# Handing an up projection over to its down projection: last column pair one tile at a time, its square and blocks in halves, a product moved forward

## The chip, the cores and the metric

The kernel runs on one core of one Trainium2 chip. The metric is the device time of one execution in microseconds. Engines are named as the profile names them: PE multiplies matrices (PEld is its weight load, which overlaps it), DVE and ACT work element by element, POOL is the general-purpose engine, SP issues most of the DMAs. Results of PE land in PSUM, in eight banks of 128 x 512 floats; the kernel names them a (two), b (two), c (two), d and e.

## The reference

A decoder trunk of two layers on 512 tokens of width 1024: a gated short convolution, then an MLP; a shared key and value side; sparse attention, then an MLP; a last normalization. The change touches the MLP alone:

```python
def squared_relu_mlp(h, w1, w2):
    return jnp.square(jax.nn.relu(h @ w1)) @ w2
```

`w1` is 1024 x 4096, `w2` 4096 x 1024, all in float32.

## The kernel before

**Numbers in two halves.** Every float32 operand is split into a float16 high half and a float16 low half. A product of two operands is three matmuls: high by high, low by high, high by low. `ACT.activation(..., AF.Copy)` makes the high half and a DVE subtraction makes the low half, for weights (`whi`/`wlo`, `wh`) as for activations (`rh` high, `rl` low).

**Stages of an MLP.** Each MLP handles the 4096 hidden channels in two halves, and each half is an up projection (`mlp_up`) followed by a down projection (`mlp_down`). So in the whole kernel there are four handovers from an up projection to a down projection: two in layer 0, two in layer 1.

**Up projection.** `mlp_up` (line 1010) goes over eight column pairs `p`. A pair is two tiles of 128 hidden channels by 512 tokens, each accumulated in its own PSUM bank. Most pairs are computed by `pair` (line 773): for each of eight chunks of the contraction it issues three matmuls for the first tile and three for the second, so both tiles are complete only at the end, after 48 matmuls of 512 columns. Its weights come as two pieces, one for chunks 0 to 3 and one for chunks 4 to 7. (In the second half some pairs, never the last one, are made by `seven` with seven products of half-size blocks.)

**`squares(p)`** (line 1023) turns a pair into what the down projection needs. DVE scales each tile and clips it at zero (`ml_t`, two instructions of 512 columns). ACT squares both in one instruction of 1024 columns (`ml_z`, blocks 0 to 3 of 256 columns: the two tiles by the two halves of the tokens). `sums_of` (line 454) makes blocks 4 to 7, differences of the first four, in three DVE instructions. Then one ACT copy of blocks 1 to 7 (1792 columns) makes `rh[:, p]`, and one DVE subtraction of 1792 columns makes `rl[:, p]`.

**Down projection.** The seven products of a Strassen-like scheme stand for the eight block products of a 2 x 2 by 2 x 2 multiplication. `PRODUCTS` (line 321) gives for each of the products 0 to 6 its weight block and its activation block: product 0 reads activation block 1, product 1 reads block 3, product 4 reads block 4. `mlp_down` (line 1062) goes over four column pairs. `product(i, ps, cs)` (line 1068) issues, for each chunk `c` of `cs`, three matmuls of 256 columns into bank `ps`; chunk `c` reads `rh[:, c]` and `rl[:, c]`, and so chunk 7 needs `squares(7)`, the last pair of the up projection. When `give` is set the product frees its weight block, and it then calls `ahead()`, which converts further weight pieces as far as there is room: the converted blocks lie in a ring of seven, and the eighth needs the tile of the first.

For the first down pair (line 1095) three products, 0 into bank a, 4 into bank c and 1 into bank d, run over chunks 0 to 6 first. After that chunk 7 of product 0 is issued, ACT copies the result of product 0 into the bank of W_ (bank b), chunk 7 of product 4 and of product 1 follow, and then product 2 accumulates on top of the copy in bank b.

**What sets the order.** The instructions of a stage are not issued as they are written. `Plan` records them as tasks, each numbered as the program came to it, with an estimated cost (`cost`) and its dependencies. `issue` (line 185) then simulates the engines and lists the tasks: on each engine, of the tasks that are ready or will be within a short look-ahead (60 ns on PE, 150 on DVE and ACT), the one with the lowest number is next. An engine that finds nothing of a low number ready takes a later task, for instance a weight conversion for a stage that comes much later; such tasks are called fillers below. The order that comes out is fixed: on the chip each engine runs its list strictly in order and waits at semaphores. Layer 0's MLP is one plan, attention another, layer 1's MLP a third.

Of the kernel before, what the change touches and what calls it, by code (L numbers as in the profile page):

```python
# [12 lines left out]
AF = mybir.ActivationFunctionType  # L13
OP = mybir.AluOpType
# [267 lines left out]
def body(ctx, tc, x, rel_bias, norm_mix, norm_mlp, mlp_w1, mlp_w2, a_w_in, a_conv_w, a_w_out,  # L282
# [4 lines left out]
    PE, ACT, DVE, POOL, SPQ = (plan.engine(e) for e in ("PE", "ACT", "DVE", "POOL", "SP"))  # L287
# [143 lines left out]
    def kind(i):  # L431
        shape = pieces[i][1]
        return "seven" if shape is None else "down" if shape[0] == "down" else "dense"

    def room(ring, n, more=1):
        return all(ring[-k]["done"] for k in range(n - more + 1, n + 1) if k <= len(ring))
# [187 lines left out]
    def next_piece():  # L624

        i = pos["use"]
        pos["use"] += 1
        while i not in ready:
            for _ in convert_piece():
                pass  # L630
        return ready.pop(i)

    def ahead():
        while pos["cv"] < len(pieces) and pos["cv"] < pos["use"] + AHEAD2[kind(pos["cv"])]:
            k = kind(pos["cv"])
            if k != "dense" and not room(halves, HALVES[0], 2 if k == "seven" else 1):
                return
            yield from convert_piece()

    def drain(gen):  # L640
        for _ in gen:
            pass


    first = tc.tile_pool(name="first", bufs=1)
# [122 lines left out]
    def mm3(ps, w, xs, start, stop):  # L768
        PE.matmul(ps, w[0], xs[0], start=start, stop=False)
        PE.matmul(ps, w[0], xs[1], start=False, stop=False)  # L770
        PE.matmul(ps, w[1], xs[0], start=False, stop=stop)

    def pair(xs, ps, kn=8, mid={}):

        for c in range(kn):
            if c % 4 == 0:
                if c:
                    drain(ahead())
                w = next_piece()
            if c in mid:  # L780
                mid[c]()
            for m in range(2):
                mm3(ps[m], [u[:, c % 4, m * 128:(m + 1) * 128] for u in w], [u[:, c] for u in xs],
                    c == 0, c == kn - 1)
# [12 lines left out]
    xs = new_split(wk[0], "x0")  # L797
# [80 lines left out]
    for p in range(4):  # L878
        pc, pu, pb = [], [], []
        if p == 0:  # L880
# [38 lines left out]
            ws = [next_piece(), next_piece()]  # L919
# [21 lines left out]
        for part, dst in ((1, pc), (2, pu), (0, pb)):  # L941
# [12 lines left out]
            for c in SUM_AT.get((p, part), ()):  # L954
                z = wk[0].tile([128, 8, 256], F32, name="sv_z", bufs=1)
                with plan.behind(first_lo[0]):
                    block_sums(c, "mix0", z, [sums[:, hl, 4 * c:4 * c + 4] for hl in range(2)])
            for m in range(2):
                ch = 2 * p + m
                if dst is pc:  # L960
                    if m == 0:
                        tmps = []
                    t = ftile("cv_t", 2)
# [23 lines left out]
    xs = new_split(work, "xs")  # L987
    ss = SumSq()
# [18 lines left out]
    ROOT_AT, ROWS_AT = 7, 1  # L1007
    SUMS_AT = (3, 4, 5, 6)

    def mlp_up(xs, ss, rh, half, rb, gname, kept):  # L1010
        turn[0], layer = 1, int(gname[-1])
        first = half == 0
        if not first:
            sums = [u[:, 5:8].rearrange("p a b n -> p (a b) n")[:, 0:16] for u in rh]
            for hl in range(2):
                POOL.dma_start(sums[hl], kept[:, hl])

        def rows():
            nonlocal rb
            rb = row_tile(broadcast_rows(ss.r), RD * math.sqrt(SR) / (SW * SX))  # L1020
            squares(0)

        def squares(p):
            ph = held[p]
            t = wk[0].tile([128, 2, S], F32, name="ml_t", bufs=2)
            if len(ph) == 3:
                lo, hi = slice(0, 256), slice(256, 512)
                DVE.scalar_tensor_tensor(t[:, :, lo], ph[0], 0.0, rb[:, None, lo].to_broadcast([128, 2, 256]),
                                         op0=OP.max, op1=OP.mult)
                for m in range(2):  # L1030
                    DVE.scalar_tensor_tensor(t[:, m, hi], ph[1 + m], 0.0, rb[:, hi], op0=OP.max, op1=OP.mult)
            else:
                for m in range(2):
                    DVE.scalar_tensor_tensor(t[:, m], ph[m], 0.0, rb, op0=OP.max, op1=OP.mult)
            z = wk[0].tile([128, 8, 256], F32, name="ml_z", bufs=2)
            ACT.activation(z[:, 0:4].rearrange("p (m k) n -> p m (k n)", m=2), t, AF.Square)
            sums_of(z)
            ACT.activation(rh[0][:, p], z[:, 1:8], AF.Copy)
            DVE.tensor_tensor(rh[1][:, p], z[:, 1:8], rh[0][:, p], op=OP.subtract)

        held = {}
        for p in range(8):
            if not first and p in UP7[layer]:
                dlo = wk[0].tile([128, 2, 256], F32, name="dn_w", bufs=1)
                held[p] = seven(xs, sums, dlo)
                drain(ahead())
                squares(p)
                continue
            held[p] = [acc(), acc()]
            pair(xs, held[p], mid={ROOT_AT: ss.rstd} if first and p == 0 else {ROWS_AT: rows} if first and p == 1 else {})  # L1050
            drain(ahead())
            if p or not first:
                squares(p)
            if first and p in SUMS_AT:
                c = SUMS_AT.index(p)
                z = wk[0].tile([128, 8, 256], F32, name="ml_z", bufs=2)
                block_sums(c, gname, z, [u[:, 7, 0:4] for u in rh])
                for hl in range(2):
                    SPQ.dma_start(kept[:, hl, 4 * c:4 * c + 4], rh[hl][:, 7, 0:4])
        return rb  # L1060

    def mlp_down(rh, done, mid=None, last=None):

        sc = 1.0 / (SR * SW2)
        n1, n2 = slice(256, 512), slice(0, 256)
        blocks = {}

        def product(i, ps, cs=range(8), more=False, give=True):
            own = more and len(cs) == 8
            a, b = PRODUCTS[i]  # L1070
            if i not in blocks:
                blocks[i] = next_piece()
            wh, wl, u = blocks[i]
            for c in cs:
                xh, xl = (r[:, c, b - 1] for r in rh)
                for n, (w, x_) in enumerate(((wh, xh), (wl, xh), (wh, xl))):
                    PE.matmul(ps, w[:, c], x_, start=not more and c == 0 and n == 0, stop=c == 7 and n == 2,
                              skip_group_check=own)
            if give:
                u["done"] = True  # L1080
            drain(ahead())

        for p in range(4):
            blocks.clear()
            if last and p == 3:
                return last(blocks, product)
            X1, X2 = X[:, 2 * p + 1], X[:, 2 * p]
            both = X[:, 2 * p:2 * p + 2, n2]
            X_, W_, V_ = (bank(g + str(p % 2))[:, 0:256] for g in "abc")

            def stt(o, ps):
                DVE.scalar_tensor_tensor(o, ps, sc, o, op0=OP.mult, op1=OP.add)

            u = wk[0].tile([128, 2, 256], F32, name="dn_w", bufs=1)
            if p == 0:
                Y_ = bank("d")[:, 0:256]
                for i, ps in ((0, X_), (4, V_), (1, Y_)):
                    product(i, ps, range(7), give=False)
                product(0, X_, (7,), True)
                ACT.activation(W_, X_, AF.Copy)  # L1100
                product(4, V_, (7,), True)
                ACT.activation(u[:, 0], V_, AF.Copy, scale=sc)
                product(1, Y_, (7,), True)
                stt(X1[:, n1], X_)
                stt(X1[:, n1], Y_)
            else:
                product(0, X_)
                ACT.activation(W_, X_, AF.Copy)
                product(4, V_)
                ACT.activation(u[:, 0], V_, AF.Copy, scale=sc)  # L1110
            if mid and p:
                mid(p)
            product(2, W_, more=True)
            ACT.activation(u[:, 1], W_, AF.Copy, scale=sc)
            product(5, V_, more=True)
            stt(X1[:, n2], V_)
            DVE.tensor_tensor(both, both, u, op=OP.add)
            product(3, W_, more=True)
            stt(X2[:, n2], W_)
            if p:  # L1120
                product(1, X_, more=True)
                stt(X1[:, n1], X_)
            product(6, W_, more=True)
            stt(X2[:, n1], W_)
            if done:
                drain(done(p))
# [12 lines left out]
    with pool("hidden_a") as hp:  # L1139
        wk[0] = hp  # L1140
        rh = first_half(hp, xs, ss, "mlp0")
        xkv = new_split(work, "xs")
        ss = SumSq()
# [12 lines left out]
    with pool("attn") as ap_:  # L1156
# [295 lines left out]
        og, parts, keep = {}, {}, {}  # L1452
# [260 lines left out]
        for i in range(len(items) + 6):  # L1713
# [11 lines left out]
            while credit > 0.0:  # L1725
                u = next(bg, "end")
# [17 lines left out]
    xs = xm  # L1744
    ss = ss2


    with pool("hidden_b") as hp:
        wk[0] = hp
        rh = first_half(hp, xs, ss, "mlp1")  # L1750
# [163 lines left out]
```

## Time and profile before

| | us |
|---|---|
| median of 3 runs | 1091.97 |
| lowest and highest of them | 1091.97, 1092.24 |
| the profiled execution, its own time | 1091.95 |
| its span, first to last instruction | 1090.2 |
| PE busy in the span | 1073.5 |
| DVE busy | 930.7 |
| ACT busy | 639.0 |

The time of the profiled execution is 1.75 us longer than its span; the profile shows only what lies in the span. Rows of the timeline give the start, the length, the engine, the line, the operation, output<-inputs by tile name, the shape and how many instructions were merged into the row; in brackets stands the engine's idle time before it and what ended it. Every instruction has line 242, since the planner issues them all from there, so the rows are told apart by tile names. The four handovers lie at about 256, 411, 850 and 1004 us of the span. Of the names: `c<-xs,whi` is an up matmul into bank c, `a<-rh,wh` and `a<-rl,wh` are down matmuls with the high and the low half of the activations, `ml_t<-c,rb` is the scaling in `squares`, `ml_z<-ml_t` its Square, `ml_z<-ml_z` its sums, `rh<-ml_z` its copy, `rl<-ml_z,rh` its subtraction, `b<-a` the copy into W_'s bank, `wh<-wst` a weight conversion.

### The profile page before, as it was taken

The page shows a single profiled execution, that of the slowest core. Times are in us where ns is not written, and L with a number is a line of the kernel's source. Part 1 is how long each engine was busy: PE and PEld are TensorE (multiplying, and loading weights), DVE is VectorE, ACT ScalarE, POOL GpSimd, SP SyncE. Part 2 cuts the span into 40 slices and gives each one's busy share as a digit, 9 for nine tenths or more (in the row PEclk, how much of TensorE's full clock was granted, in tenths as well). Part 3 has the DMA queues.
Part 4 walks back from the last instruction along what each step waited for, and adds up shares of the span by engine and source line. Part 5 has one row for each costly group of instructions (what it writes and reads, how often), then busy time and mean ns, then how long its engine had stood idle before and what let it go on. Part 6 is the DMA issues. An engine that isn't in the chain of part 4 may idle for free.

```text
span 1090.2 us, 21151 instructions
## 1 busy us (share of the span) xinstructions
PE 1073.5 (98%) x8442; PEld 736.7 (68%) x8442; DVE 930.7 (85%) x1574; ACT 639.0 (59%) x1082; POOL 68.4 (6%) x93
## 2 busy tenths in 40 slices
PE   9999999999999999999999999999999999999997
PEld 4457844446885758886766696775444788775887
DVE  7999987899986898958886889997879996699883
ACT  6655555566543565546766687865656543554552
POOL 2000000000000000000002122210000000000121
PEclk9999999999999999999999999999999999999999
DMA  8535698345425414215633352002834453431312
GB/s 273 174 106 171 231 286 278 112 155 156 136 78 174 147 47 137 77 37 152 195 116 117 99 194 67 22 21 76 233 117 136 135 155 107 153 119 45 112 40 78
DMA packets 159236, 143.45 MB, mean 132 GB/s; under 512 B 7853, under 2 KB 147841, under 8 KB 158625
## 3 DMA queue, kind: packets, MB, share of 16 engines
q1 hardware_dynamic: 155712, 132.60, 39.6%
q10 hardware_dynamic: 2464, 4.70, 1.3%
q0 software_dynamic: 960, 4.80, 1.2%
q8 instruction: 66, 1.08, 0.4%
q14 instruction: 34, 0.27, 0.1%
HBM read 123.55 MB, written 15.51 MB: 128 GB/s over the span
## 4 chain that ended last, share of the span: by engine, by line
PE 78%; DVE 16%; issue 2%; ACT 2%; DMA 1%; SPq 0%; POOL 0%; POOLq 0%; DVEq 0%; ACTq 0%
PE b L242 28%; PE a L242 26%; PE c L242 20%; DVE ml_z L242 3%; DVE rl L242 3%; PE d L242 3%; DVE ml_t L242 3%; DVE wh L242 3%; DVE wlo L242 2%; PE e L242 1%; ACT rh L242 1%; DVE wst L242 1%; DMA wst<-a_w_in_dram 1%; ACT ml_z L242 0%; DVE at_s L242 0%
## 5 line engine op out<-in xcount | busy, mean ns | idle before, releaser
L242 PEld LDWEIGHTS <-wh 128*128 128x128 f16 x3648 | 356.3, 98 | 54.6 <-ACT wh L242 4.8
L242 PEld LDWEIGHTS <-whi 128*128 128x128 f16 x1664 | 159.9, 98 | 165.2 <-issue 1.8
L242 PE MATMUL b<-rh,wh 128*128 128x256 f16 x904 | 151.6, 273 | 0.5 <-ACT b L242 0.5
L242 ACT ACTIVATE whi<-wst 128x1024 f16<-128x1024 f32 (+5 forms) x122 | 103.1, 858 | 76.5 <-PE b L242 29.5
L242 PEld LDWEIGHTS <-wlo 128*128 128x128 f16 x832 | 81.4, 98 | 88.9 <-DVE wlo L242 0.6
L242 ACT ACTIVATE wh<-wst 128x1024 f16<-128x1024 f32 (+1 forms) x108 | 106.3, 1005 | 59.7 <-PE b L242 32.9
L242 DVE SCALAR_TENSOR_TENSOR wlo<-wst,whi 128x1024 f16<-128x1024 f32 (+5 forms) x122 | 118.1, 980 | 24.4 <-ACT whi L242 24.3
L242 DVE SCALAR_TENSOR_TENSOR wh<-wst,wh 128x1024 f16<-128x1024 f32 (+1 forms) x108 | 123.3, 1164 | 5.0 <-ACT wh L242 3.2
L242 PE MATMUL b<-rl,wh 128*128 128x256 f16 x452 | 123.2, 273 | 0.0
L242 PE MATMUL a<-xs,whi 128*128 128x512 f16 (+1 forms) x384 | 103.1, 355 | 0.1
L242 PE MATMUL b<-xs,whi 128*128 128x512 f16 x320 | 95.3, 379 | 0.0
L242 PE MATMUL c<-rh,wh 128*128 128x256 f16 x552 | 93.6, 273 | 0.0
L242 ACT ACTIVATE at_p<-at_s,at_m 128x128 f32<-128x128 f32 (+3 forms) x128 | 71.0, 556 | 29.0 <-DVE at_m L242 27.1
L242 ACT ACTIVATE rh<-ml_z 128x1792 f16<-128x1792 f32 (+1 forms) x40 | 62.7, 1567 | 42.2 <-DVE ml_z L242 42.2
L242 DVE TENSOR_TENSOR rl<-ml_z,rh 128x1792 f16<-128x1792 f32 (+1 forms) x40 | 74.4, 1861 | 15.1 <-ACT rh L242 15.0
L242 PE MATMUL c<-xs,whi 128*128 128x512 f16 x288 | 86.0, 379 | 0.0
L242 ACT ACTIVATE wh<-ml_t 128x1024 f16<-128x1024 f32 x48 | 50.6, 1054 | 48.7 <-DVE ml_t L242 45.5
L242 PE MATMUL a<-rh,wh 128*128 128x256 f16 x432 | 73.3, 273 | 3.7 <-ACT wh L242 3.7
L242 PE MATMUL c<-rl,wh 128*128 128x256 f16 x276 | 75.2, 273 | 0.0
L242 DVE CUSTOM_DVE_ANT_0 at_s<-b,T 128x128 f32<-128x128 f32 (+3 forms) x128 | 59.1, 485 | 15.1 <-PE b L242 14.4
L242 PE MATMUL a<-xs,wlo 128*128 128x512 f16 (+1 forms) x192 | 67.4, 355 | 0.0
L242 DVE TENSOR_TENSOR ml_z<-ml_z 128x256 f32<-128x256 f32 (+1 forms) x120 | 61.5, 512 | 5.1 <-ACT ml_z L242 2.2
(294 smaller groups left out, 2004.7 us busy)
## 6 DMA issues: line engine op xcount, KB each, us to landing
wst<-mlp_w_dram SPq DMA_DIRECT2D x32, 1024.0 KB, 5.4
wst<-mlp_w_dram SPq DMA_DIRECT2D x100, 256.0 KB, 3.8
early<-pre_hl SPq DMA_DIRECT2D x14, 512.0 KB, 3.6
wst<-mlp_w_dram SPq DMA_DIRECT2D x48, 128.0 KB, 2.7
wst<-a_w_in_dram SPq DMA_DIRECT2D x20, 256.0 KB, 4.0
wst<-w_kv_dram SPq DMA_DIRECT2D x10, 512.0 KB, 4.0
T<-ext_d ACTq DMA_DIRECT2D x4, 1056.0 KB, 6.1
wst<-a_w_in_dram SPq DMA_DIRECT2D x8, 512.0 KB, 5.0
```

The lines of the kernel that those rows point to most:

```text
L242: getattr(self.engines[t["e"]], t["op"])(*t["args"], **t["kw"])
```

## The change

Three edits, all at the handover. A new function `pair_in_turn` takes both weight pieces of the pair at its start and issues all 24 matmuls of the first tile and then all 24 of the second; further weight conversions are recorded after the fourth chunk of each. `mlp_up` uses it for `p == 7`.

For `p == 7` `squares` makes the Square in two instructions of 512 columns, one for each tile. The ACT copy is made in two parts: blocks 1 to 3 ahead of `sums_of`, blocks 4 to 7 after it. The DVE subtraction is split in the same way, and both of its parts are recorded after `sums_of`.

In `mlp_down`, for the first down pair, products 0 and 4 run over chunks 0 to 6, then chunk 7 of product 0, ACT's copy into W_, product 1 over all eight chunks, and only then chunk 7 of product 4.

```diff
+    def pair_in_turn(xs, ps):
+
+        ws = [next_piece(), next_piece()]
+        for m in range(2):
+            for c in range(8):
+                if c == 4:
+                    drain(ahead())
+                mm3(ps[m], [u[:, c % 4, m * 128:(m + 1) * 128] for u in ws[c // 4]], [u[:, c] for u in xs],
+                    c == 0, c == 7)
...
-            ACT.activation(z[:, 0:4].rearrange("p (m k) n -> p m (k n)", m=2), t, AF.Square)
+            for k in [slice(m, m + 1) for m in range(2)] if p == 7 else [slice(0, 2)]:
+                ACT.activation(z[:, 0:4].rearrange("p (m k) n -> p m (k n)", m=2)[:, k], t[:, k], AF.Square)
+            parts = (slice(1, 4), slice(4, 8)) if p == 7 else (slice(1, 8),)
+            if p == 7:
+                ACT.activation(rh[0][:, p, 0:3], z[:, 1:4], AF.Copy)
             sums_of(z)
-            ACT.activation(rh[0][:, p], z[:, 1:8], AF.Copy)
-            DVE.tensor_tensor(rh[1][:, p], z[:, 1:8], rh[0][:, p], op=OP.subtract)
+            for k in parts:
+                to = slice(k.start - 1, k.stop - 1)
+                if p < 7 or k.start == 4:
+                    ACT.activation(rh[0][:, p, to], z[:, k], AF.Copy)
+                DVE.tensor_tensor(rh[1][:, p, to], z[:, k], rh[0][:, p, to], op=OP.subtract)
...
-            pair(xs, held[p], mid={ROOT_AT: ss.rstd} if first and p == 0 else {ROWS_AT: rows} if first and p == 1 else {})
+            (pair_in_turn if p == 7 else pair)(xs, held[p], **{} if p == 7 else dict(mid={ROOT_AT: ss.rstd} if first and p == 0 else {ROWS_AT: rows} if first and p == 1 else {}))
...
-                for i, ps in ((0, X_), (4, V_), (1, Y_)):
+                for i, ps in ((0, X_), (4, V_)):
                     product(i, ps, range(7), give=False)
                 product(0, X_, (7,), True)
                 ACT.activation(W_, X_, AF.Copy)
+                product(1, Y_)
                 product(4, V_, (7,), True)
                 ACT.activation(u[:, 0], V_, AF.Copy, scale=sc)
-                product(1, Y_, (7,), True)
                 stt(X1[:, n1], X_)
                 stt(X1[:, n1], Y_)
```

## The prediction, made before the changed kernel was run

> **What bounds the kernel now.** The page comes first, for the engine that has no room; then the busy time by stretches, for the places where that engine does stand still; then the timeline of those places.
>
> ```profile
> span 1090.2 us, 21151 instructions
> PE 1073.5 (98%) x8442; PEld 736.7 (68%) x8442; DVE 930.7 (85%) x1574; ACT 639.0 (59%) x1082; POOL 68.4 (6%) x93
> ```
>
> ```profile
> 256.00:266.30 10.30, 8.72 (x76) 7.19 (x75) 10.23 (x13) 5.32 (x6) 0.00 (x0) 1.00 0.55 177
> 266.30:330.00 63.70, 63.70 (x584) 57.06 (x584) 58.59 (x75) 30.45 (x38) 0.00 (x0) 1.00 0.40 118
> 330.00:411.00 81.00, 81.00 (x509) 49.50 (x508) 68.41 (x87) 42.09 (x44) 1.15 (x2) 1.00 0.40 129
> 411.00:420.70 9.70, 8.69 (x76) 7.17 (x75) 8.34 (x12) 4.19 (x5) 0.00 (x0) 1.00 0.61 200
> ...
> 1004.00:1014.10 10.10, 9.00 (x78) 7.34 (x77) 7.08 (x10) 4.24 (x5) 0.00 (x0) 1.00 0.68 210
> ```
>
> The columns are the stretch, its length, then busy time and count of PE, PEld, DVE, ACT and POOL, then the granted clock, DMA share and GB/s. PE is the bound: in a down projection (266 to 330) and an up half (330 to 411) it is busy for every microsecond. The short stretches are the four handovers from an up projection to the first down pair; there PE loses time. A busy row counts a matmul's whole duration, which overlaps the next, so the loss is better read from starts:
>
> ```profile
> 263.53 0.38 PE L242 MATMUL d<-rh,wh 128*128 128x256 f16 x2
> 264.39 0.27 PE L242 MATMUL a<-rl,wh 128*128 128x256 f16 x1 [0.48 <-DVE rl L242]
> 264.50 0.27 PE L242 MATMUL c<-rl,wh 128*128 128x256 f16 x1
> 264.61 0.27 PE L242 MATMUL d<-rl,wh 128*128 128x256 f16 x1
> 265.81 0.28 PE L242 MATMUL a<-rh,wh 128*128 128x256 f16 x1 [0.93 <-ACT wh L242]
> 266.26 0.38 PE L242 MATMUL b<-rh,wh 128*128 128x256 f16 x2 [0.17 <-ACT b L242]
> ...
> 418.49 0.38 PE L242 MATMUL d<-rh,wh 128*128 128x256 f16 x2
> 418.96 0.27 PE L242 MATMUL a<-rl,wh 128*128 128x256 f16 x1
> ...
> 420.64 0.38 PE L242 MATMUL b<-rh,wh 128*128 128x256 f16 x2
> ...
> 857.60 0.38 PE L242 MATMUL d<-rh,wh 128*128 128x256 f16 x2
> 858.46 0.27 PE L242 MATMUL a<-rl,wh 128*128 128x256 f16 x1 [0.48 <-DVE rl L242]
> ...
> 860.33 0.38 PE L242 MATMUL b<-rh,wh 128*128 128x256 f16 x2 [0.17 <-ACT b L242]
> ...
> 1011.96 0.38 PE L242 MATMUL d<-rh,wh 128*128 128x256 f16 x2
> 1012.23 0.27 PE L242 MATMUL a<-rl,wh 128*128 128x256 f16 x1
> ...
> 1014.10 0.38 PE L242 MATMUL b<-rh,wh 128*128 128x256 f16 x2 [0.17 <-ACT b L242]
> ```
>
> ```profile
> 269.04 2.62 PE c L242 x24
> ...
> 194.22 10.36 PE a L242 x48
> ```
>
> 24 matmuls of 256 columns take 2.62 us, 0.109 each. Between the two quoted starts of a handover lie six of them, 0.66 us. So PE stands still for 2.73 - 0.66 = 2.07 us at the first handover, 2.15 - 0.66 = 1.49 at the second, 2.73 - 0.66 = 2.07 at the third, 2.14 - 0.66 = 1.48 at the fourth: **7.11 us in all**. It has two parts. The first wait, for the low halves `rl` of the last pair, is 264.39 - 263.75 = 0.64 at the first handover. The second (265.81 - 264.72 = 1.09, and 266.26 - 265.92 = 0.34) is for ACT, which first splits a weight block and only then copies X_ into W_'s bank. At the others the first wait is the distance from `d<-rh` to `a<-rl` less two matmuls, 0.47 - 0.22 = 0.25, 0.86 - 0.22 = 0.64 and 0.27 - 0.22 = 0.05. The second wait is the remainder: 1.43, 1.24, 1.43 and 1.43. Sums: 1.58 for the first wait, 5.53 for the second.
>
> **The change, part by part.** These are the two helpers at the first handover:
>
> ```profile
> 257.43 1.06 ACT L242 ACTIVATE ml_z<-ml_t 128x1024 f32<-128x1024 f32 x1 [3.01 <-DVE ml_t L242]
> ...
> 260.21 1.70 ACT L242 ACTIVATE rh<-ml_z 128x1792 f16<-128x1792 f32 x1 [0.59 <-DVE ml_z L242]
> 264.70 1.06 ACT L242 ACTIVATE wh<-wst 128x1024 f16<-128x1024 f32 x1 [2.79 <-PE a L242]
> ...
> 254.98 1.22 DVE L242 SCALAR_TENSOR_TENSOR wh<-ml_t,wh 128x1024 f16<-128x1024 f32 x1
> 256.12 1.28 DVE L242 SCALAR_TENSOR_TENSOR ml_t<-c,rb 128x512 f32<-128x512 f32 x2
> 257.31 1.22 DVE L242 TENSOR_TENSOR wst<-wst 128x1024 f32<-128x1024 f32 x1
> 258.52 1.61 DVE L242 TENSOR_TENSOR ml_z<-ml_z 128x512 f32<-128x512 f32 x3
> ...
> 261.19 1.22 DVE L242 SCALAR_TENSOR_TENSOR wlo<-wst,whi 128x1024 f16<-128x1024 f32 x1
> 262.32 2.02 DVE L242 TENSOR_TENSOR rl<-ml_z,rh 128x1792 f16<-128x1792 f32 x1
> ...
> 260.80 0.38 PE L242 MATMUL d<-rh,wh 128*128 128x256 f16 x2
> ```
>
> ```profile
> L242 DVE TENSOR_TENSOR rl<-ml_z,rh 128x1024 f16<-128x1024 f32 x8 | 9.8, 1220 | 0.0
> ...
> L242 ACT ACTIVATE rh<-ml_z 128x1024 f16<-128x1024 f32 x8 | 8.4, 1053 | 8.2 <-DVE ml_z L242 8.2
> ...
> L242 DVE TENSOR_TENSOR ml_z<-ml_z 128x512 f32<-128x512 f32 x40 | 27.5, 688 | 2.4 <-ACT ml_z L242 2.2
> ...
> L242 ACT ACTIVATE sq<-X 128x512 f32<-128x512 f32 x21 | 13.0, 621 | 7.3 <-DVE X L242 6.7 <-DVE ssacc L242 0.4
> ```
>
> *The fourth product moved.* Now the program runs products 0 and 4 over seven chunks, closes product 0, lets ACT split the block that frees and copy X_ to W_, and meanwhile runs product 1 whole (2.62 us) and the end of product 4 (3 x 0.109 = 0.33). That is 2.95 us of matmuls beside 1.06 + 0.37 us on ACT with their hops, the 1.65 us that lie between 264.61 and 266.26. The second wait goes at all four handovers: **-5.5 us**. Nothing is late next: product 2 then finds its bank 1.3 us early. No matmul and no DMA is added; product 1 already had its weight block as third of the ring of seven, and SP's and POOL's queues are not passed.
>
> *Two tiles in turn.* The same 48 matmuls, 24 and 24 instead of threes. No row shows 24 of 512 columns in one bank; the 256-column row above does so at 0.109, half of 10.36 / 48 = 0.216, so I take nothing (bounds: 0, and 0.1 us a handover if the turn costs one gap). The second weight piece is needed 2.6 us into the pair instead of 5.2; its lower half is split before the pair starts, so this is free:
>
> ```profile
> 237.13 1.22 DVE L242 SCALAR_TENSOR_TENSOR wlo<-wst,whi 128x1024 f16<-128x1024 f32 x1
> ...
> 245.85 0.59 PE L242 MATMUL c<-xs,whi 128*128 128x512 f16 x2
> ```
>
> The first tile is finished about 5.2 us before the second, and its scaling by DVE could run then. At the first and third handover it hardly will: the planner takes the lowest number that is ready, weight splits and the pair before have lower ones, and DVE runs without a pause up to 256.12. So I leave both scalings where they are.
>
> *Square and blocks in halves.* Before: scalings until 257.4, Square 1.06, filler on DVE until 258.5, sums until 260.1, copy of seven blocks 1.70 until 261.91, then a filler holds DVE to 262.32, and `rl` ends at 264.34. After, estimated from the rows: the second half of Square, 0.62 as the 512-column `sq`, ends at about 258.05; the copy of three blocks (768 columns, between 0.62 and 1.05, I take 0.84) ends at 258.9, beside the sums, which the filler holds where they were, until 260.1. The subtraction of 768 columns, between 0.69 for 512 and 1.22 for 1024, I take 0.95, ends at 261.05. Product 0's last chunk starts at 260.80 with two matmuls that need only `rh`, and wants `rl` at 261.02. The rest: copy of 1024 columns (1.05) from 260.2 to 261.25, at worst one filler of 1.22 on DVE, subtraction 1.22 until 263.5; product 4's last chunk wants it at 261.13 + 2.62 = 263.75. So the first wait goes too, **-1.6 us**, with 0.25 us to spare in the second half and none in the first. Should the first be late, product 1's 21 ready matmuls, 2.29 us, can be put before it: the planner issues what is ready. Added work, one Square, one copy and one subtraction more at each handover, lies beside matmuls; with that cover gone the subtraction would cost between 0.69 + 1.22 - 2.02 = -0.11 us (768 columns as cheap as 512) and 0.95 + 1.22 - 2.02 = 0.15 us.
>
> [...]
>
> *Sum.* 7.11 us less, of which I give back 0.15 for the first half having no room: 1091.95 (this profiled execution, 1.75 over its span) - 6.96 = **1085.0**. The runs' median is 1091.97, the same to 0.02. All this is PE time, and PE is full in the stages that follow a handover, so an earlier start is kept if its feeders follow.
>
> **Rivals.** (1) The split gains nothing where DVE is full: the first waits at the first and third stay, 2 x 0.64, so 1084.84 + 1.28 = 1086.1. For it: no pause on DVE before 256.12 and two fillers in the chain. Against it: the 1792-column row is cut to 768 ahead of the wait.
>
> (2) The feeders don't follow: DVE is busy 58.59 of 63.70 us in the down projection, and it loses some 2 us of filler time at a handover. If half the gain becomes waits for weight splits, 1091.95 - 3.55 = 1088.4. Against it: PE is never idle there and 5 us of DVE are.
>
> (3) The change doesn't do what it says of the second wait: ACT, with more pieces to run, copies X_ to W_ late again and all 5.53 come back: 1090.4. Against it: it would need 1.3 us more on an ACT that is busy 5.32 of 10.30.
>
> (4) **Slower.** Product 1 was the cover of the `rl` wait. If the planner leaves it behind product 0's last chunk and `rl`'s first part comes no earlier than the whole does now (264.39), PE waits from 261.02, 3.37 us, instead of 2.07: 1.30 worse, the same at the third: 25 matmuls, 2.73 us, would no longer lie before the wait, and behind it stand product 1 on PE and, through the block that product 0 frees, ACT's split and copy. The second is 0.25 + 2.73 - 1.49 = 1.49 and the fourth 0.05 + 2.73 - 1.48 = 1.30 worse. Sum 5.4: 1097.3. It loses from the point where that part is later than 261.02 + 2.07 = 263.1, against an expected 261.05. Against it: fixed order by readiness, and two microseconds of room.
>
> **How the numbers follow.** Forecast (1084.2 to 1085.8) 0.50; rival 1, 0.20; rival 2, 0.12; rival 3, 0.06; rival 4, 0.05; more than the stalls, by a reshuffled plan that also removes a wait elsewhere, below 1084.2, 0.07. About 0.2% (2.2 us) is what a measurement of this kernel can tell from no change, so faster means below 1089.8: 0.50 + 0.20 + 0.07 and most of rival 2, 0.11, is 0.88; rival 3 and the rest, 0.07, is the same; slower 0.05. The range leaves out rivals 3 and 4 and the tails of the others: 1083.6 to 1089.0.
>
> **What would show it.** In the profile after, at each handover: product 1's matmuls in bank d between the last of bank a and the last of bank c; no PE idle before bank b, and ACT's weight split and copy beside bank d (first step). `rl` in two parts, the first ended before PE wants it (third step); the first tile's scaling early at the second and fourth handover alone. PE busy 100% in every stretch between handovers (the sum). I am wrong if PE waits at product 0's last chunk, if a wait for `wh` appears in the down projections, or if the plan moves work so that one tile of 24 waits for its weights.

## The result, and the profile after

The changed kernel takes 1084.95 us, the median of four runs (1084.27 to 1085.48); beside it the kernel before took 1092.02 (1091.97 to 1092.24). The ratio is 0.9935, with a 95% interval of 0.9917 to 0.9952, so 7.07 us less. The profiled execution took 1084.27 us. One execution of all those told of here, one of e2 below, ran at a granted clock of 0.65 and took 1606.6 us; medians and ratios are of the others.

The page of the changed kernel, its span and the busy time of the engines:

```profile
span 1082.5 us, 21160 instructions
PE 1071.9 (99%) x8442; PEld 737.5 (68%) x8442; DVE 928.6 (86%) x1578; ACT 640.1 (59%) x1090; POOL 69.4 (6%) x93
```

PE issues the same 8442 matmuls in a span that is 7.7 us shorter; ACT has eight instructions more and DVE four. The changed kernel by stretches (start and end, length, then busy time and count of PE, PEld, DVE, ACT and POOL, granted clock, DMA share, GB/s), with the first handover in row 1, the down projection behind it in row 2, and the second, third and fourth handover in rows 3, 4 and 5 (dots stand where rows are left out):

```profile
255.40:263.60 8.20, 8.20 (x76) 7.20 (x74) 8.13 (x11) 5.41 (x7) 0.00 (x0) 1.00 0.30 100
263.60:327.40 63.80, 63.80 (x587) 57.18 (x585) 60.37 (x78) 30.48 (x38) 0.00 (x0) 1.00 0.45 134
...
408.40:416.50 8.10, 8.10 (x75) 7.16 (x74) 8.03 (x10) 3.86 (x5) 0.00 (x0) 1.00 0.72 233
844.00:852.20 8.20, 8.20 (x66) 6.36 (x65) 8.13 (x11) 6.12 (x9) 0.00 (x0) 1.00 0.39 128
998.00:1006.20 8.20, 8.20 (x74) 7.13 (x73) 7.18 (x10) 3.86 (x5) 0.00 (x0) 1.00 0.79 259
```

The first handover held 76 matmuls in 10.30 us before and holds 76 in 8.20 now. PE is busy for all of every row, and read by starts no gap is left at any of the four handovers. The feeders follow: DVE is busy 60.37 of 63.80 us in the down projection and PE still loses nothing there.

All 7.11 us of the stalls are gone. The two profiled executions differ by 7.68. Most of the other 0.57 lies ahead of the first handover: the first matmul of the down projection starts at 256.21 us before and at 255.68 after, and in the experiments, whose kernels are alike up to the last column pair, anywhere from 255.5 to 256.7; the changed kernel itself has 255.68 in this execution and 256.04 in another (e0 below). PE's gaps lie in the first 25 us (busy 22.54 us of them before, 23.38 after), and from 25 to 60 us it is busy throughout in both. So it is no part of the change, and the difference of the medians is 7.07.

The timeline of the changed kernel at the first handover, and below the dots at the second, PE alone:

```profile
260.26 0.38 PE L242 MATMUL a<-rh,wh 128*128 128x256 f16 x2
260.48 0.27 PE L242 MATMUL a<-rl,wh 128*128 128x256 f16 x1
260.59 0.38 PE L242 MATMUL d<-rh,wh 128*128 128x256 f16 x2
...
263.21 0.38 PE L242 MATMUL c<-rh,wh 128*128 128x256 f16 x2
263.43 0.27 PE L242 MATMUL c<-rl,wh 128*128 128x256 f16 x1
263.54 0.38 PE L242 MATMUL b<-rh,wh 128*128 128x256 f16 x2
...
413.13 0.38 PE L242 MATMUL a<-rh,wh 128*128 128x256 f16 x2
413.35 0.38 PE L242 MATMUL d<-rh,wh 128*128 128x256 f16 x2
413.56 0.27 PE L242 MATMUL d<-rl,wh 128*128 128x256 f16 x1
413.67 0.27 PE L242 MATMUL a<-rl,wh 128*128 128x256 f16 x1
```

Bank a closes, product 1 runs in bank d, bank c closes, bank b begins. No row has a bracket for idle time. At the second handover the planner put three matmuls of bank d ahead of the last one of bank a, the reshuffle that the prediction allowed for.

The helpers at the first handover of the changed kernel:

```profile
257.59 0.84 ACT L242 ACTIVATE rh<-ml_z 128x768 f16<-128x768 f32 x1
258.34 1.04 ACT L242 ACTIVATE wh<-wst 128x1024 f16<-128x1024 f32 x1
259.58 1.06 ACT L242 ACTIVATE rh<-ml_z 128x1024 f16<-128x1024 f32 x1 [0.20 <-DVE ml_z L242]
260.79 0.37 ACT L242 ACTIVATE b<-a 128x256 f32<-128x256 f32 x1
261.07 1.05 ACT L242 ACTIVATE wh<-wst 128x1024 f16<-128x1024 f32 x1
...
257.94 1.61 DVE L242 TENSOR_TENSOR ml_z<-ml_z 128x512 f32<-128x512 f32 x3
259.47 0.95 DVE L242 TENSOR_TENSOR rl<-ml_z,rh 128x768 f16<-128x768 f32 x1
...
261.47 1.22 DVE L242 TENSOR_TENSOR rl<-ml_z,rh 128x1024 f16<-128x1024 f32 x1
```

The first part of `rl` ends at 259.47 + 0.95 = 260.42, and PE's first matmul with it starts at 260.48. The second ends at 262.69, and PE wants it at 263.43. One thing here is not as foretold: ACT copies X_ into W_'s bank (`b<-a`, 260.79) **before** it splits the freed weight block (`wh<-wst`, 261.07), where before it was the other way round, the split at 264.70 and then the copy:

```profile
265.84 0.37 ACT L242 ACTIVATE b<-a 128x256 f32<-128x256 f32 x1
```

So bank b is ready at 260.79 + 0.37 = 261.16 in the changed kernel, 2.4 us before it is wanted.

### The profile page after: what moved, and what is told of

Read it like the earlier page. It is cut to its first block, busy times and chain, and to the rows that moved or that the text cites. A ratio compares the mean times of both kernels' runs of the same rounds, so it can differ in the third digit from the quotient of the medians.

```text
span 1082.5 us, 21160 instructions
## 1 busy us (share of the span) xinstructions
PE 1071.9 (99%) x8442; PEld 737.5 (68%) x8442; DVE 928.6 (86%) x1578; ACT 640.1 (59%) x1090; POOL 69.4 (6%) x93
## 4 chain that ended last, share of the span: by engine, by line
PE 97%; DVE 2%; issue 0%; ACT 0%; POOL 0%; POOLq 0%; DVEq 0%; ACTq 0%
PE b L242 34%; PE a L242 31%; PE c L242 27%; PE d L242 4%; PE e L242 1%; DVE at_s L242 0%; DVE wh L242 0%; DVE at_pl L242 0%; DVE xs L242 0%; DVE big L242 0%; DVE o_t L242 0%; POOL rfin L242 0%; DVE VT L242 0%; ACT x L242 0%; POOLq L1927 0%
## 5 line engine op out<-in xcount | busy, mean ns | idle before, releaser
L242 ACT ACTIVATE rh<-ml_z 128x1792 f16<-128x1792 f32 (+2 forms) x44 | 63.5, 1443 | 40.1 <-DVE ml_z L242 40.0
L242 DVE TENSOR_TENSOR rl<-ml_z,rh 128x1792 f16<-128x1792 f32 (+2 forms) x44 | 75.1, 1706 | 12.8 <-ACT rh L242 12.8
```

The costliest lines, as they stand in the source:

```text
L242: getattr(self.engines[t["e"]], t["op"])(*t["args"], **t["kw"])
```

## The experiments

A stall is read as in the prediction, from PE's starts in the profile of each kernel, at all four handovers. Where a kernel has a wait some 10 us further on, at the second product in bank b (0.2 to 0.3 us at the first and third handover, about 0.1 at the fourth), it is counted too. e1 to e4 ran beside runs of the kernel before with a median of 1091.64, e5, e7, e8 and e9 beside 1092.02, e0, e6 and e10 beside 1091.72.

| kernel | median us | ratio to before, 95% interval | stalls of PE, us |
|---|---|---|---|
| before | 1091.64 to 1092.02 | | 7.11 |
| e0_after: the change | 1084.56 | 0.9933 (0.9920 to 0.9945) | 0 |
| e1_move_only | 1088.65 | 0.9971 (0.9961 to 0.9982) | 3.85 |
| e2_split_turn | 1088.64 | 0.9970 (0.9958 to 0.9982) | 3.61 |
| e3_no_turn | 1085.06 | 0.9936 (0.9923 to 0.9948) | 0 |
| e4_copy_first | 1088.55 | 0.9971 (0.9960 to 0.9982) | 3.83 |
| e5_move_pinned | 1100.60 | 1.0079 (1.0063 to 1.0096) | 15.38 |
| e6_square_whole | 1084.92 | 0.9936 (0.9924 to 0.9949) | 0 |
| e7_blocks_whole | 1087.81 | 0.9959 (0.9945 to 0.9974) | 3.23 |
| e8_split_copy_first | 1084.64 | 0.9929 (0.9914 to 0.9944) | 0 |
| e9_split_ahead_of_copy | 1084.94 | 0.9932 (0.9917 to 0.9947) | 0 |
| e10_blocks_copy_first | 1084.61 | 0.9932 (0.9919 to 0.9946) | 0 |

### The moved product alone (e1_move_only)

The kernel before with the change's last edit and nothing else:

```diff
-                for i, ps in ((0, X_), (4, V_), (1, Y_)):
+                for i, ps in ((0, X_), (4, V_)):
...
+                product(1, Y_)
...
-                product(1, Y_, (7,), True)
```

> Only product 1 is moved; square, blocks and the last pair are as before. Sum theory (the prediction's sum: product 1 is cover for ACT, the second wait of 5.53 us goes with the move alone, the first wait of 1.58 stays): 1092.0 - 5.5 = 1086.5 us. Order theory (the planner pulls product 1's ready chunks ahead of product 0's last chunk, which still waits for rl, so product 1 is no cover there; what the move does by itself is that ACT's copy into bank b is recorded ahead of the weight split): first wait stays 0.64, 0.25, 0.64, 0.05; second wait shrinks from 1.43 to the copy and its hops, about 0.4; about 1.0 us at each handover, 1088.0 us. Cover theory (without the split the cover is used up and nothing else changes): 1092.0 us.

It gains 2.99 us by the medians. PE of this kernel at the first handover, then ACT:

```profile
264.16 0.38 PE L242 MATMUL c<-rh,wh 128*128 128x256 f16 x2
264.84 0.27 PE L242 MATMUL a<-rl,wh 128*128 128x256 f16 x1 [0.30 <-DVE rl L242]
265.06 0.27 PE L242 MATMUL c<-rl,wh 128*128 128x256 f16 x1
265.57 0.38 PE L242 MATMUL b<-rh,wh 128*128 128x256 f16 x2 [0.24 <-ACT b L242]
...
265.15 0.37 ACT L242 ACTIVATE b<-a 128x256 f32<-128x256 f32 x1 [2.79 <-PE a L242]
265.43 1.05 ACT L242 ACTIVATE wh<-wst 128x1024 f16<-128x1024 f32 x1
```

Two things follow. The cover that the prediction counted on isn't there: `rl` comes late, so the planner spends product 1's ready matmuls ahead of `a<-rl`, and only two matmuls of product 1 and product 4 stand between that and bank b. What the move does change is ACT's order: the copy goes ahead of the weight split, and the second wait falls from 1.43 to 0.40 (265.57 - 265.06 = 0.51, less 0.11 for the matmul that starts at 265.06). The order theory's 1088.0 left out a wait ten microseconds on, 0.31 us at the first and the third handover and 0.08 at the fourth.

### The order on ACT alone (e4_copy_first)

Why does the order on ACT turn? `ahead()` converts pieces only up to a fixed number beyond those that the program has taken. When product 0 is closed in the moved order, product 1's block isn't taken yet, so the split into the freed tile isn't recorded until product 1 has taken its block, behind the copy. This kernel records it behind the copy directly, and keeps the old order of the products:

```diff
-                product(0, X_, (7,), True)
+                product(0, X_, (7,), True, give=False)
                 ACT.activation(W_, X_, AF.Copy)
+                blocks[0][2]["done"] = True
+                drain(ahead())
```

> The kernel before with one edit: ACT's copy of product 0 into bank b is recorded ahead of the weight split that the freed block allows. Products, pair, square and blocks as before. Order theory: first wait stays, second wait falls from 1.43 to about 0.4 (copy 0.37 and hops) at each handover: about 1088.1 us. Sum theory (only matmuls beside ACT's work end the second wait): no change, 1092.0 us.

ACT of this kernel at the first handover:

```profile
263.98 0.37 ACT L242 ACTIVATE b<-a 128x256 f32<-128x256 f32 x1 [2.79 <-PE a L242]
264.26 1.05 ACT L242 ACTIVATE wh<-wst 128x1024 f16<-128x1024 f32 x1
```

It gains 3.09 us, and its four stalls, 1.35, 0.65, 1.36 and 0.47, are those of e1 (1.37, 0.64, 1.36, 0.48) to 0.02. So without the split the moved product is worth what the place of one 0.37 us copy in ACT's list is worth, and the place of the matmuls adds nothing to it that can be read.

### The split without the move (e2_split_turn)

The changed kernel with the order of the products of before, that is, without the last hunk of the diff.

> Only the last pair in turn and the halves of square and blocks; products in the order of before. Sum theory: the first wait of 1.58 us goes, the second stays whole: 1090.4 us. Order theory: the first wait goes, and product 0's last chunk is issued in one piece, 4 matmuls or 0.44 us earlier than before, so ACT's split and copy start that much earlier; second wait about 1.0 each: 1092.0 - 1.58 - 4 x 0.44 = 1088.7 us.

It gains 3.00 us, where the prediction gave these edits 1.6. PE of this kernel at the first handover, then ACT:

```profile
263.29 0.27 PE L242 MATMUL a<-rl,wh 128*128 128x256 f16 x1
263.94 0.27 PE L242 MATMUL d<-rl,wh 128*128 128x256 f16 x1
264.71 0.28 PE L242 MATMUL a<-rh,wh 128*128 128x256 f16 x1 [0.49 <-ACT wh L242]
265.08 0.38 PE L242 MATMUL b<-rh,wh 128*128 128x256 f16 x2
...
263.60 1.06 ACT L242 ACTIVATE wh<-wst 128x1024 f16<-128x1024 f32 x1 [2.48 <-PE a L242]
264.66 0.37 ACT L242 ACTIVATE b<-a 128x256 f32<-128x256 f32 x1
```

The first wait is gone at all four handovers, as foretold. But the second shrank as well. Before, PE issued the `rh` matmuls of banks a, c and d while it waited for `rl`, so that only `c<-rl` and `d<-rl` were left behind `a<-rl`. Now bank a closes first, and the whole last chunks of c and d, six matmuls, lie beside ACT: four matmuls or 0.44 us more cover at each handover, 1.76 us in all. At the first and the third the copy also starts 0.08 us sooner behind the start of the weight split (264.66 - 263.60 = 1.06, before 265.84 - 264.70 = 1.14). ACT's order is the old one, and 3.61 us of the second wait are left.

### The two routes to the rest (e8_split_copy_first, e9_split_ahead_of_copy)

e8 has the split, the old order of the products, no turn, and ACT's copy first as in e4.

> Square and blocks in halves, no turn, products in the order of before, and ACT's copy into bank b recorded ahead of the weight split; product 1 isn't moved. Order theory: after product 0's last chunk 7 matmuls, 0.77 us, lie beside the copy and its hops, 0.73 us, so both waits go: 1085.1 us. Cover theory (product 1 has to lie beside ACT's work): the second wait stays as in e2, 1088.7 us.

e9 is the changed kernel with the weight split recorded ahead of the copy again:

```diff
+                blocks[1] = next_piece()
                 product(0, X_, (7,), True)
                 ACT.activation(W_, X_, AF.Copy)
                 product(1, Y_)
```

> The changed kernel, but product 1's weight block is taken before product 0 is closed, and by that ACT splits the freed block ahead of its copy into bank b, as in the kernel before. Cover theory (as the prediction had it): 2.95 us of matmuls hide 1.65 us of ACT: 1085.0 us. If only the order on ACT counts: the second wait comes back with about 1.1 us a handover, 1089.4 us.

Neither has a stall left, and their intervals hold the change's ratio. In e9, ACT and then PE at the first handover:

```profile
261.80 1.06 ACT L242 ACTIVATE wh<-wst 128x1024 f16<-128x1024 f32 x1 [0.18 <-PE a L242]
262.76 0.37 ACT L242 ACTIVATE b<-a 128x256 f32<-128x256 f32 x1
...
264.54 0.38 PE L242 MATMUL b<-rh,wh 128*128 128x256 f16 x2
```

Here the late copy ends at 263.13, 1.4 us before bank b begins: the cover that the prediction described, working as it said. In e8 there is no such cover, but ACT needs only the copy. So once `rl` is early, either ends the second wait: the matmuls between, or the order on ACT. The change has both, and one is idle.

### The other edits (e3_no_turn, e6_square_whole, e7_blocks_whole)

e3 is the changed kernel with `pair` kept for the last pair:

```diff
-            (pair_in_turn if p == 7 else pair)(xs, held[p], **{} if p == 7 else dict(
+            pair(xs, held[p], mid=
```

> All of the change but the turn: the last pair's tiles alternate by threes as before. If the turn does nothing (at the first and third handover DVE has no room for the early scaling, at the second and fourth there is slack): as the changed kernel, 1085.0 us, no PE wait at a handover. If the early scaling is needed where DVE had room: up to 0.6 us more at the second and fourth handover, 1086.2 us.

e6 has the Square whole again:

```diff
-            for k in [slice(m, m + 1) for m in range(2)] if p == 7 else [slice(0, 2)]:
-                ACT.activation(z[:, 0:4].rearrange("p (m k) n -> p m (k n)", m=2)[:, k], t[:, k], AF.Square)
+            ACT.activation(z[:, 0:4].rearrange("p (m k) n -> p m (k n)", m=2), t, AF.Square)
```

> All of the change, but Square in one instruction of 1024 columns again. If DVE's filler holds the sums anyway (it ended at 258.53 in the kernel before, Square at 258.49), the halved square gains nothing: 1085.0 us, no wait at a handover. If it counts: Square ends 0.44 us later, rl's first part too, and PE waits some 0.4 us at each handover: 1086.6 us.

e7 has the seven blocks copied and subtracted at once again:

```diff
-            parts = (slice(1, 4), slice(4, 8)) if p == 7 else (slice(1, 8),)
-            if p == 7:
-                ACT.activation(rh[0][:, p, 0:3], z[:, 1:4], AF.Copy)
+            parts = (slice(1, 8),)
```

> All of the change, but the copy and the subtraction of the seven blocks are whole again; turn, halved square and moved product stay. If rl's first part is what frees product 0's last chunk: rl comes as late as before, the planner pulls product 1 forward, and the time is that of e1, 1088.6 us. If the halved square is what matters: 1085.0 us.

While the blocks are split, nothing is lost that can be measured without the turn or with the Square whole (1085.06 and 1084.92, no stall). Without the split of the blocks 3.23 us of stalls come back, and the median is 2.87 above that of e9, which ran beside it. PE of e7 from the first handover on:

```profile
263.91 0.27 PE L242 MATMUL a<-rl,wh 128*128 128x256 f16 x1 [0.19 <-DVE rl L242]
...
264.64 0.38 PE L242 MATMUL b<-rh,wh 128*128 128x256 f16 x2 [0.24 <-ACT b L242]
...
274.56 0.38 PE L242 MATMUL b<-rh,wh 128*128 128x256 f16 x2 [0.15 <-DVE X L242]
```

The rows show `rl` late, then the copy late because bank a closed late, and ten microseconds on a wait for DVE, which was pushed back too. By starts the stalls are 1.30 at the first handover, 0.57 at the second, 1.29 at the third and 0.07 at the fourth. That is 0.62 less than in e1, most of it at the fourth handover (0.48 there): DVE's sums wait 1.12 us for the Square in the kernel before, whose Square and blocks are those of e1, and 0.70 in e7. So the turn and the halved Square do gain a little where the blocks are whole, and nothing beside their split.

### The smallest edit, and the change again (e10_blocks_copy_first, e0_after)

e10 is the kernel before with the blocks split and ACT's copy first; the Square is whole, the tiles are not in turn and no product is moved.

> The smallest version that the runs so far point to: blocks copied and subtracted in two parts, ACT's copy into bank b recorded ahead of the weight split; Square whole, last pair alternating, products in the order of before. If rl's first part and the order on ACT are all that is needed: 1085.0 us, as the changed kernel. If square or turn or the moved product have a share after all: 1085.6 us or more, with a wait at a handover.

> The changed kernel itself, beside the two below on the same chip: 1085.0 us, no PE wait at a handover.

They are the same: 1084.61 and 1084.56. ACT and then PE of e10 at the first handover:

```profile
263.22 0.37 ACT L242 ACTIVATE b<-a 128x256 f32<-128x256 f32 x1 [2.36 <-PE a L242]
...
263.67 0.38 PE L242 MATMUL b<-rh,wh 128*128 128x256 f16 x2
```

The copy ends at 263.59 and bank b begins at 263.67: these two edits do the whole work of the change, with 0.08 us between here where the change has 2.4. No kernel of the study beats the changed one by more than the measurement can tell.

### The slower rival, built (e5_move_pinned)

e1 with product 1 held behind the last matmul of product 0, so that the planner can't use it as a cover of the `rl` wait:

```diff
-                product(0, X_, (7,), True)
+                closed = product(0, X_, (7,), True)
                 ACT.activation(W_, X_, AF.Copy)
+                product(1, Y_, after=closed)
```

> As e1 (product 1 moved, nothing split), but product 1's matmuls are held behind product 0's last one, so that the planner can't pull them forward. This is the mechanism of the slower rival. By the prediction's working PE waits for rl from the end of the seven chunks and product 1 comes after that: 1092.0 + 5.4 = 1097.3 us. Worked out with the order that the planner makes of it (product 4's last chunk is partly ahead of the wait): PE reaches bank b about 1.1 us later than before at three handovers and 1.3 at the second, 1092.0 + 4.5 = 1096.5 us. If cover is of no account: 1088.6 us as e1.

It is slower, 1.0079, and 8.58 us by the medians, where rival 4 came to 5.4. The stretches of e5 just behind the wait at the first, the second and the fourth handover:

```profile
264.00:267.00 3.00, 3.00 (x28) 2.69 (x28) 3.00 (x4) 1.33 (x2) 0.00 (x0) 1.00 1.12 330
...
419.90:423.20 3.30, 3.30 (x17) 2.31 (x17) 1.65 (x2) 1.33 (x2) 0.00 (x0) 0.50 0.00 0
...
1017.40:1020.40 3.00, 3.00 (x15) 2.06 (x14) 3.00 (x4) 1.33 (x2) 0.00 (x0) 0.50 0.03 5
```

Behind the wait at the second and the fourth handover PE got half its clock: 17 matmuls in 3.30 us against 28 in 3.00 behind the first. By starts, fifteen steps of a matmul fill the 3.20 us from 419.97 to 423.17, 0.213 each. Sixteen at 0.213 instead of 0.109 are, by estimate, 1.7 us at each of the two, 3.3 of the 15.38. Without them the stalls grew by 15.38 - 7.11 - 3.3 = 5.0 us, near rival 4's 5.4. So rival 4 was a real danger with the right sign, and its price left the clock out.

## Why the prediction was right in sum and wrong in its parts

**What bounds the kernel** was right: 7.11 us of PE at the four handovers, and all of it came off the end, since PE has next to no room in the stages behind them (before, it was busy for 277.87 of the 280 us from 486 to 766, the least full of the long ones). The medians fell by 7.07. That the median lies 0.05 us from the forecast is luck: the four runs spread over 1.2 us. The 0.15 us given back for the first half of `rl` wasn't needed: the subtraction of 768 columns took 0.95 as estimated and ended 0.06 us ahead of its use.

**The step that failed** is *The fourth product moved* with its -5.5 us, and with it the -1.6 us of *Square and blocks in halves*. The prediction shared the stalls out by what the timeline named as the releaser of each, ACT for the second wait, and gave each edit the wait it seemed aimed at. The runs share them out otherwise. By stalls, the split without the move is worth 7.11 - 3.61 = 3.50 (e2): the 1.58 of the first wait, and 1.92 of the second, 1.76 of it because bank a closes ahead of four more matmuls. The move is worth what e2 has left, 3.61, on top of the split, and 7.11 - 3.85 = 3.26 by itself (e1). By the medians the two edits are worth 3.00 and 2.99 alone. The sum holds since the parts cover the same 7.11 us between them.

**The mechanism of the move** was half right. The cover of 2.95 us is real where `rl` is early, and enough alone (e9). Without the split it isn't there at all (e1), since the planner spends it on the first wait. And the move does something that the prediction didn't see: it turns ACT's order, and that too is enough where the split is in (e8, e10). The sign to look for, "ACT's weight split and copy beside bank d", was met, with the two in the other order. The reading of `ahead()` would have told it: what is recorded depends on which blocks the program has taken so far.

**Two tiles in turn: nothing** was right for the change (e3). The first tile's scaling did come early at the second and fourth handover alone, and it gained nothing there. The halved Square was costed as a part of the chain that ends the first wait; it is not needed (e6). At the first three handovers a filler of 1.22 us holds the sums on DVE, in the kernel before as in the change; at the fourth the sums do wait for the whole Square, 1.12 us in the kernel before, but there the first part of `rl` has room (in the change it ends at 1002.57, and PE wants it at 1003.26) and PE doesn't wait.

**Rival 1**, that the split gains nothing where DVE is full, fell, and by more than the result shows: e7 loses 1.30 and 1.29 at the first and third handover, where DVE is full (busy for 10.23 of 10.30 us and 10.33 of 10.40 in the kernel before), and 0.57 and 0.07 at the others. The split paid most beside that full DVE. It costs that engine 0.95 + 1.22 - 2.02 = 0.15 us and takes more than a microsecond from what PE waits for.

**Rival 2** fell: the feeders followed. **Rival 3**, the copy late again, didn't occur in the change. The wait it names is the one that e2 keeps. **Rival 4** had two conditions. In the change the first one is met at the first handover: product 1 stands behind product 0's last chunk (bank d from 260.59, behind `a<-rl` at 260.48). The other isn't: `rl`'s first part is there at 260.42. So here the split of the blocks keeps the rival off. Where `rl` is late the planner does: e1 moves the product and lets the planner put ready matmuls ahead of the wait, and gains; e5 forbids that, and loses 8.58.

## What to carry to other kernels

Before giving an edit the wait that it is aimed at, follow what else it reorders: here a copy of 0.37 us that changed places with a 1.06 us weight split in ACT's list was worth 3 us by itself (3.09 in e4), and one edit's cover was spent on another edit's wait. Parts that add up to the right sum say nothing of each part; each edit alone, and the change without it, do. On the way to a waiting engine, cut the piece that it needs first out of a large operation even where the helper has no room to spare: at the first handover DVE was busy for 10.23 of 10.30 us.

## What the runs showed of the hardware

One thing was not expected. In e5 the clock granted to PE fell behind a wait, and only at two handovers of four: it was 0.50 from 419.90 to 423.20 and from 1017.40 to 1020.40, and 1.00 behind the wait at the first and the third (264.00 to 267.00 and 862.30 to 865.00). It isn't the longer wait that does it. The starts of PE at the first and the second handover of e5:

```profile
261.56 0.38 PE L242 MATMUL a<-rh,wh 128*128 128x256 f16 x2 [1.02 <-ACT rh L242]
263.99 0.27 PE L242 MATMUL a<-rl,wh 128*128 128x256 f16 x1 [1.83 <-DVE rl L242]
...
417.76 0.38 PE L242 MATMUL a<-rh,wh 128*128 128x256 f16 x2 [0.98 <-ACT rh L242]
419.82 0.36 PE L242 MATMUL a<-rl,wh 128*128 128x256 f16 x1 [1.46 <-DVE rl L242]
```

At the first it stood still for 1.02 + 1.83 = 2.85 us with four matmuls between, and kept its clock; at the second for 0.98 + 1.46 = 2.44, also with four, and lost half of it. Why the clock fell behind the one and not behind the other, no run here shows. For the price of a wait: at the second handover of e5 two gaps, of 1.14 and 1.62 us by starts, cost 1.7 us beyond their own length, the estimate above from sixteen matmuls at 0.213 instead of 0.109.
